# A one-core encoder layer: h turned by VectorE ahead of the gate, the gate's weight laid out piece by piece

## The chip, the cores and the metric

The kernel runs on one core of a Trainium2 chip. PE (TensorE) multiplies matrices, DVE (VectorE), ACT (ScalarE) and POOL (GpSimd) work on tiles, SP (SyncE) mostly issues transfers (DMAs). Each engine goes through its own instructions in order. The time is the device time of one execution in microseconds (us); less is better.

## The reference

One layer of a streaming encoder on 2048 + 32 rows of 1024 channels, in float32:

```
hn = rmsnorm(h, g_mix);  proj = hn @ w_in            # 1024 -> 3072
yA, yB = short gated convolution, pooling mixer      # of proj's six parts
h = h + concat([yA, yB]) @ w_out                     # 1024 x 1024
gate = sigmoid(rmsnorm(h, g_ple) @ w_ple_gate)       # 1024 x 1024
h = h + (p @ w_ple) * gate                           # p: 256 channels
return rmsnorm(h, g_final), states
```

## The kernel before

Rows come in 17 tiles: 16 of 128 rows, taken in eight pairs (0, 2, .. 14), and a short one of 32 rows (tile 16, "ol" and "gl" in names). A float32 product is made of three products of pieces: `split` (L77, L78) has ACT round a tile to its high piece and DVE subtract it for the low one. A pair's 256 x 1024 by 1024 x 1024 product is done by `seven` as seven products (the Strassen-Winograd scheme) instead of eight, each of twelve matmuls for each half. The operands of these seven are named 11, 12, 22 and S1 to S4; sums of them are tiles `fS` (L193) on DVE. Each result stays in a PSUM bank (X, Y, Z) until DVE has taken it up: `carry` makes `c_o` or `c_g` from it, `out` adds it to the row tile.

The stages, one after another:

1. The input projection and the mixers, whose result goes to DRAM transposed (`y_d`); then three early tiles of the embedding product.
2. W_out's stage. For each pair: `load_y` (L314) two y tiles, `frame_parts` makes the operands, `load_rows` (L327) the rows x, `seven` with `h_ops` (L1234) adds the product to x, `done_h` (L1260) takes the sum of squares (its root on POOL) and stores h into `h_d` on SP's queue. Meanwhile `scale_gate` (L1284 to 1289) loads the gate's weight through POOL's queue, scales it on ACT and writes `g_d`. The short tile stands between pairs 12 and 14 and goes through `plain`, whose packed products have no seven. `layout` (L1305, L1306) put W_out into its slots at the beginning.
3. The embedding stage: for 13 tiles of p, `embed`'s `prep` transposes p on PE (`ptp`, L130) and splits it, `run` multiplies it (`embed_product`, L102) and stores e into `e_d`. During it the gate's weight is read back from `g_d` (L1382) and laid out in slots of its own ("wg": `quarters`, `whole_quarters`, `weight_sums`).
4. The gate's stage, the short tile first, then the pairs. `seven` gets h as operand in transposed form. The first tile of a pair (`turned`, L1388 to 1398) is loaded from `h_d`, copied by ACT into another order (`ho`, L1394) and transposed by eight PE instructions into PSUM (`pth`, L1396). The second (`turned_here`) is loaded by four DMAs in blocks (L1405) and transposed by DVE within blocks of 32 x 32 (L1407). `prep_g` makes the operands of pair i + 2 during pair i. `gate_ops` (L1416 to 1428) applies the gate, `done_g` (L1433 to 1436) the final norm at the end of each pair, and stores the output. Pair 14 is `last_pair`.

The order on each engine is made by a scheduler which follows the program; `tc.keep_in_program_order` fixes an instruction's place, `between` hooks work into numbered steps of `seven`. Tiles come from pools with a fixed number of buffers: a new tile takes a buffer once its former tile's last reader is done, and its load waits for that. `ya` has five buffers of 128 x 1024 for y, the embedding rows and the gate's h; `xh` has three for x or h; `qa` two halves; `ring4` takes a 128 x 1024 tile from a pool.

## Time and profile before

| | us |
|---|---|
| median of 3 runs (lowest to highest) | 937.44 (936.55 to 938.89) |
| the profiled execution | 935.15 |
| its span, first to last instruction | 933.4 |
| busy in the span: PE, DVE, ACT, POOL | 917.5, 716.9, 482.2, 126.3 |

A row of the profile names an instruction or a group by its line, its engine, its operation and the tiles out<-in; numbers of buffers are left out, so `x_o` is the X bank of any W_out pair, `x_g` that of a gate pair. In brackets stands how long the engine was idle just before it, and what ended that. In the chain, "x24" is a run of 24 matmuls of one form. A table by stage gives the busy time of each engine in a stretch, with the instructions in brackets, the granted clock of TensorE (PEclk), the mean busy share of the DMA engines and the rate they moved.

### The profile page before, as it was taken

The page shows a single profiled execution, that of the slowest core. Times are in us where ns is not written, and L with a number is a line of the kernel's source. Part 1 is how long each engine was busy: PE and PEld are TensorE (multiplying, and loading weights), DVE is VectorE, ACT ScalarE, POOL GpSimd, SP SyncE. Part 2 cuts the span into 40 slices and gives each one's busy share as a digit, 9 for nine tenths or more (in the row PEclk, how much of TensorE's full clock was granted, in tenths as well). Part 3 has the DMA queues.
Part 4 walks back from the last instruction along what each step waited for, and adds up shares of the span by engine and source line. Part 5 has one row for each costly group of instructions (what it writes and reads, how often), then busy time and mean ns, then how long its engine had stood idle before and what let it go on. Part 6 is the DMA issues. An engine that isn't in the chain of part 4 may idle for free.

```text
span 933.4 us, 13100 instructions
## 1 busy us (share of the span) xinstructions
PE 917.5 (98%) x4581; PEld 827.8 (89%) x4581; DVE 716.9 (77%) x1215; ACT 482.2 (52%) x895; POOL 126.3 (14%) x244
## 2 busy tenths in 40 slices
PE   8999999899999999999999999999999999999996
PEld 7999999899999999999999987888878868888885
DVE  7997988989577868585777679665564798888985
ACT  7734564644445554443545446344334875555664
POOL 3111132211001110000000011111211001211113
PEclk9999999999999999999999999999999999999999
DMA  9357587597945547328656359766775884566563
GB/s 266 84 157 221 182 269 223 182 290 259 415 134 153 161 155 206 123 87 278 199 169 175 127 194 289 251 184 196 222 228 174 321 270 121 206 225 233 194 208 113
DMA packets 133791, 190.05 MB, mean 204 GB/s; under 512 B 11740, under 2 KB 101084, under 8 KB 132445
## 3 DMA queue, kind: packets, MB, share of 16 engines
q1 hardware_dynamic: 117741, 138.78, 47.5%
q0 software_dynamic: 13248, 44.93, 14.8%
q10 hardware_dynamic: 2736, 5.51, 1.8%
q8 instruction: 36, 0.59, 0.3%
q14 instruction: 30, 0.25, 0.1%
HBM read 129.59 MB, written 59.58 MB: 203 GB/s over the span
## 4 chain that ended last, share of the span: by engine, by line
PE 75%; DMA 2%; ACT 2%; issue 1%; DVE 1%; POOL 0%; POOLq 0%; DVEq 0%; ACTq 0%
PE x_o L167 9%; PE x_g L167 9%; PE x_zab L577 5%; PE e L102 5%; PE z_g L167 5%; PE z_o L167 4%; PE x_ch L577 4%; PE x_zbv L577 4%; PE z_zab L577 2%; PE y_g L167 2%; PE z_ch L577 2%; PE y_o L167 2%; PE b L577 2%; PE z_zbv L577 2%; PE c L577 2%; PE v L577 2%
## 5 line engine op out<-in xcount | busy, mean ns | idle before, releaser
L77 ACT CAST y_S<-y_fS 128x512 fp32r<-128x512 f32 x32 | 19.5, 622 | 43.7 <-PE x_o L167 19.2
L102 PE MATMUL e<-wq,pps 128*128 128x512 f32 (+1 forms) x156 | 38.9, 399 | 0.2 <-ACT pps L77 0.2
L167 PE MATMUL x_g<-wg_b,g_S 128*128 128x512 f32 x128 | 35.9, 390 | 0.0
L167 PE MATMUL x_o<-wo_b,y_S 128*128 128x512 f32 x128 | 35.8, 391 | 0.0
L577 PE MATMUL x_zab<-B,w_zab_S 128*128 128x416 f32 x168 | 34.6, 353 | 1.0 <-DVE w_zab_S L78 0.7
L577 PE MATMUL z_ch<-B,w_ch_S 128*128 128x416 f32 x168 | 34.3, 352 | 0.9 <-ACT U L973 0.9
L577 PE MATMUL z_zab<-B,w_zab_S 128*128 128x416 f32 x168 | 34.1, 351 | 0.5 <-ACT U L973 0.5
L577 PE MATMUL x_zbv<-B,w_zbv_S 128*128 128x416 f32 x168 | 34.2, 352 | 0.3 <-ACT zs L973 0.3
L577 PE MATMUL z_zbv<-B,w_zbv_S 128*128 128x416 f32 x168 | 34.2, 352 | 0.0
L577 PE MATMUL x_ch<-B,w_ch_S 128*128 128x416 f32 x168 | 34.1, 351 | 0.0
L102 PEld LDWEIGHTS e<-wq,pps 128*128 128x128 f32 (+1 forms) x156 | 27.4, 182 | 6.9 <-ACT pps L77 0.5
L577 PEld LDWEIGHTS x_zab<-B,w_zab_S 128*128 128x128 f32 x168 | 31.1, 188 | 2.2 <-DVE w_zab_S L78 1.0
L577 PEld LDWEIGHTS z_ch<-B,w_ch_S 128*128 128x128 f32 x168 | 31.2, 188 | 1.6 <-ACT U L973 1.2
L577 PEld LDWEIGHTS z_zab<-B,w_zab_S 128*128 128x128 f32 x168 | 31.3, 188 | 1.1 <-ACT U L973 0.8
L577 PEld LDWEIGHTS x_zbv<-B,w_zbv_S 128*128 128x128 f32 x168 | 31.3, 188 | 1.0 <-ACT zs L973 0.6
L577 PEld LDWEIGHTS x_ch<-B,w_ch_S 128*128 128x128 f32 x168 | 31.3, 188 | 0.5 <-ACT c_s L973 0.2
L577 PEld LDWEIGHTS z_zbv<-B,w_zbv_S 128*128 128x128 f32 x168 | 31.3, 188 | 0.4
L69 POOL TENSOR_SCALAR ms_f<-ssq_f 128x1 f32<-128x1 f32 (+1 forms) x15 | 8.8, 588 | 160.7 <-ACT junk L88 160.7
L77 ACT CAST y<-y 128x512 fp32r<-128x512 f32 x24 | 14.9, 620 | 28.7 <-PE z_o L167 12.8
L1435 DVE SCALAR_TENSOR_TENSOR h<-h,rstd_f,g_bc 128x1024 f32<-128x1024 f32 (+1 forms) x15 | 19.3, 1284 | 12.7 <-POOL rstd_f L73 12.7
L412 DVE SCALAR_TENSOR_TENSOR xt<-xt,rstd_x,g_bc 128x1024 f32<-128x1024 f32 (+2 forms) x14 | 17.9, 1282 | 13.9 <-POOL rstd_x L73 12.7
L167 PEld LDWEIGHTS x_o<-wo_b,y_S 128*128 128x128 f32 x128 | 24.0, 188 | 5.1 <-ACT c_o L1239 0.3
(583 smaller groups left out, 2662.5 us busy)
## 6 DMA issues: line engine op xcount, KB each, us to landing
y<-y_d SPq DMA_DIRECT2D x16, 512.0 KB, 10.2
x<-in_x_prompt_dram SPq DMA_DIRECT2D x16, 512.0 KB, 6.2
h_d<-x SPq DMA_DIRECT2D x16, 512.0 KB, 4.2
h<-h_d SPq DMA_DIRECT2D x16, 512.0 KB, 3.7
xt<-in_x_prompt_dram SPq DMA_DIRECT2D x15, 512.0 KB, 6.8
e<-e_d SPq DMA_DIRECT2D x15, 512.0 KB, 5.8
out_dram<-h POOLq DMA_DIRECT2D x14, 512.0 KB, 3.0
p_dT<-T POOLq DMA_DIRECT2D x12, 512.0 KB, 6.2
```

The lines of the kernel that those rows point to most:

```text
L69: nc.gpsimd.tensor_scalar(ms[:n], ssq[:n], scalar1=1.0 / D, scalar2=EPS, op0=ALU.mult, op1=ALU.add)
L77: ins = nc.scalar.copy(hi, src)
L102: nc.tensor.matmul(ps[:n], pps[:, a, k, :n], wp[k][b][:, cs], start=k + q == 0, stop=k == 1 and q == 2)
L167: nc.tensor.matmul(ps[:n], lhs[:, k, a, :n], w[b][:, k], start=start and k + q == 0, stop=k == KH - 1 and q == 2, skip_group_check=True)
L412: nc.vector.scalar_tensor_tensor(xt[:n], xt[:n], r[:n], g_bc[:n], op0=ALU.mult, op1=ALU.mult)
L577: nc.tensor.matmul(ps[:, :NB], lhs[:, k, x], b[:, k, y], start=start and k + q == 0, stop=stop and k == KH - 1 and q == 2, skip_group_chec ...
L1435: nc.vector.scalar_tensor_tensor(h[:n], h[:n], rf[:n], g_bc[:n], op0=ALU.mult, op1=ALU.mult)
```

## The change

- In W_out's stage each finished h tile is transposed within blocks by DVE (`turn_h`), the first of a pair at step 6 of its `seven`, the second at step 1 of the next pair, and stored on POOL's queue by four DMAs into new DRAM tiles `t_d` and `t_s`, block by block, so that the whole tile lies there transposed. `turned` in the gate's stage is then one load; the PE transposes, ACT's copies and the gate stage's DVE transposes are gone.
- `ya` is divided into `ya` with three buffers and `yb` with two, which holds the turned tiles, the embedding rows and others; `qa` holds one full tile. The y tiles of the next pair are loaded ahead of `seven`, after the x rows.
- The gate's weight is laid out into W_out's own slots, piece by piece, as they come free, from loads spread over `ya` and `xh`.
- `done_g` of a pair runs at step 1 of the next pair (`norms`).
- The embedding's p tiles are loaded two at a time; the first two are prepared at steps 3 and 4 of W_out's pair 14; the order of the last three is changed to 13, 16, 14, and the product of tile 14 is issued within the short gate tile, at `between` in `plain`.

The diff, cut to its core:

```diff
--- before.py
+++ after.py
@@ -43,6 +44,8 @@
     e_d = tc.dram_tile([T, D], F32, name="e_d")
+    t_d = tc.dram_tile([SEQ // P, P, D], F32, name="t_d")
+    t_s = tc.dram_tile([P, D // 4], F32, name="t_s")
     g_d = tc.dram_tile([D, D], F32, name="g_d")
@@ -96,12 +99,14 @@
-    def embed_product(ps, pps, wp, cs, n=P):
+    def embed_product(ps, pps, wp, cs, n=P, later=False):
         for k in range(2):
             for q, (a, b) in enumerate(((0, 0), (0, 1), (1, 0))):
-                nc.tensor.matmul(ps[:n], pps[:, a, k, :n], wp[k][b][:, cs], start=k + q == 0, stop=k == 1 and q == 2)
-
-    def embed(todo, wp, ring, queue=nc.sync):
+                ins = nc.tensor.matmul(ps[:n], pps[:, a, k, :n], wp[k][b][:, cs], start=k + q == 0, stop=k == 1 and q == 2)
+                if later:
+                    tc.keep_in_program_order(ins)
+
+    def embed(todo, wp, ring, queue=nc.sync, some=4, ahead=2):
@@ -132,18 +137,17 @@
-        def run(c, last=False):
+        def run(c, last=False, later=False):
             i = todo[c]
             r, n = tiles[i]
-            prep(c)
-            prep(c + 1)
-            prep(c + 2)
+            for a in range(ahead + 1):
+                prep(c + a)
             pps = got[c]
...
                 ps = bank(f"e_{i}_{nh}")
-                embed_product(ps, pps, wp, cs, n)
+                embed_product(ps, pps, wp, cs, n, later)
                 (nc.vector.tensor_copy if last and nh else nc.scalar.copy)(o[:n, cs], ps[:n])
@@ -272,7 +276,7 @@
-    def plain(name, A, W, n, carry, out):
+    def plain(name, A, W, n, carry, out, between=lambda: None):
@@ -280,6 +284,7 @@
         out(Z, c2, (0, 1))
+        between()
         packed(X, A[1], W["21"], n, False)
@@ -1180,12 +1185,12 @@
                 nc.sync.dma_start(g_bc, g_fin.partition_broadcast(P))
-                ya = ctx.enter_context(tc.tile_pool(name="ya", bufs=5, side="right"))
+                ya, yb = (ctx.enter_context(tc.tile_pool(name=n, bufs=b, side="right")) for n, b in (("ya", 3), ("yb", 2)))
                 first_y = load_y(0, 2 * P)
-                first_x = load_rows(ya, "x", 0, x_p)
-                tops = [ring4(ya, f"wo_q{i}") for i in range(2)]
+                tops = [ring4(yb, f"wo_q{i}") for i in range(2)]
                 for k in range(KH):
                     load_top(k, tops[k // 2])
+                first_x = load_rows(ya, "x", 0, x_p)
             if gi == 1:
@@ -1215,7 +1220,7 @@
         w3, qa, xh, st, ss, cmb = (pool(*a) for a in (
-            ("w3", 1), ("qa", 2), ("xh", 3), ("st", 4), ("ss", 3), ("cmb", 8)))
+            ("w3", 1), ("qa", 1), ("xh", 3), ("st", 4), ("ss", 3), ("cmb", 8)))
@@ -1259,8 +1264,18 @@
-        def prep_h(i):
-            lo, hi = load_y(i, 2 * P) if i else first_y
+        def turn_h(i, x):
+
+            r, n = tiles[i]
+            t = ring4(yb, f"ht_{i}")
+            tc.keep_in_program_order(nc.vector.transpose(t[:n], x[:n]))
+            g = n // 32
+            to = (t_d[i] if g == 4 else t_s).rearrange("(q c) (g n) -> g c q n", q=4, g=g)
+            for b in range(g):
+                nc.gpsimd.dma_start(to[b], t[b * 32:b * 32 + 32].rearrange("c (q n) -> c q n", q=4))
+
+        def prep_h(i, y):
+            lo, hi = y
             S[i], more = frame_parts(cmb, ss, f"y{i}", lo[:, :, :P], hi[:, :, :P], lo[:, :, P:], hi[:, :, P:])
@@ -1278,7 +1293,8 @@
-            ts = [qa.tile([P, NH], F32, tag="q", name=f"gs_{k}_{half}") for half in range(2)]
+            t = qa.tile([P, D], F32, tag="q", name=f"gs_{k}")
+            ts = t[:, :NH], t[:, NH:]
             rows = w_gate.rearrange("(q k c) n -> k q c n", q=4, k=KC)[k]
@@ -1313,8 +1329,21 @@
+
+        rest_e = [*range(EARLY, NT - 3), NT - 1, NT - 3]
+
+        def ring(what, i):
+            if what == "pps":
+                return st.tile([P, 2, 2, P], F32R, tag="t", name=f"pps_{i}")
+            if what == "out" and i not in rest_e[-LATE:]:
+                return cmb.tile([P, D], F32, tag="c", name=f"eout_{i}")
+            return ring4(yb, f"eout_{i}") if what == "out" else ss.tile([P, 2 * PLE], F32, tag="s", name=f"ep_{i}")
+
+        wq = []
+        prep, run = embed(rest_e, wq, ring, some=2)
+
         S = {}
-        more = prep_h(0)
+        more = prep_h(0, first_y)
         gate_rows = iter(range(KC))
@@ -1327,23 +1356,34 @@
                 x = [load_rows(xh, "x", i + b, x_p) for b in range(2)] if i else [first_x, second_x]
-            seven(f"o{i}", S.pop(i), W, *h_ops(x, P, f"o{i}", i == 0), {0: {1: rest}, 2: {3: next_gate}}.get(i, {}), True, i == 0)
-            for b in range(2):
-                done_h(i + b, x[b])
+                if i + 2 < NT - 1:
+                    y = load_y(i + 2, 2 * P)
+            def first_done():
+                done_h(i, x[0])
+                turn_h(i, x[0])
+
+            steps = {1: rest if i == 0 else turn_second, 3: next_gate if i == 2 else lambda: None, 6: first_done}
+            if i + 2 == NT - 1:
+                steps.update({3: partial(prep, 0), 4: partial(prep, 1)})
+            seven(f"o{i}", S.pop(i), W, *h_ops(x, P, f"o{i}", i == 0), steps, True, i == 0)
+            done_h(i + 1, x[1])
+            turn_second = partial(turn_h, i + 1, x[1])
             last = i + 4 == NT - 1
...
                 n = tiles[NT - 1][1]
-                A = short("yl", load_y(NT - 1, n), n)
+                A = short("yl", [t[:, :, :n] for t in load_y(NT - 1, n)], n)
             if i + 2 < NT - 1:
...
                 with tc.issue_after(loaded[-1].ins), tc.issue_after(hold[-1].ins):
-                    more = prep_h(i + 2)
+                    more = prep_h(i + 2, y)
                 more()
...
                 done_h(NT - 1, x)
+                turn_h(NT - 1, x)
             next_gate()
+        turn_second()
@@ -1357,55 +1397,27 @@
-        wp = embedding_chunks("wq")
-
-        rest_e = [*range(EARLY, NT - 2), NT - 1]
-
-        def ring(what, i):
-            if what == "pps":
-                return st.tile([P, 2, 2, P], F32R, tag="t", name=f"pps_{i}")
-            if what == "out" and i not in rest_e[-LATE:]:
-                return cmb.tile([P, D], F32, tag="c", name=f"eout_{i}")
-            return ring4(ya, f"e{what}_{i}")
-
-        _, run = embed(rest_e, wp, ring)
+        wq.extend(embedding_chunks("wq"))
         for c in range(len(rest_e) - LATE):
...
-        W = sums_slots("wg")
-        quarters("wg", W)
+
         for k in range(KH):
-            raw = [ring4(xh, f"wg_r{k}_{i}") for i in range(2)]
+            raw = [ring4(t, f"wg_r{k}_{i}") for i, t in enumerate(((ya, xh), (ya, ya), (xh, xh), (ya, xh))[k])]
             for i in range(2):
...
-        def turned(i):
+        def turned(i, pool=ya):
             r, n = tiles[i]
-            t = load_rows(ya, "hn", i, h_d).rearrange("p (q k c) -> p k q c", q=4, k=KC)
-            out = []
-            for half in range(2):
-                pt = tbank(f"pth_{i}_{half}")
-                o = qa.tile([P, KH, P], F32, tag="q", name=f"ho_{i}_{half}")
-                nc.scalar.copy(o[:n].rearrange("p k (q c) -> p k q c", q=4), t[:n, half * KH:half * KH + KH])
-                for k in range(KH):
-                    nc.tensor.transpose(pt[:, k * P:k * P + n], o[:n, k], ident[:n, :n])
-                out.append(pt.rearrange("p (k t) -> p k t", k=KH))
-            return out
-
-        def turned_here(i):
-
-            r, n = tiles[i]
-            t = ring4(ya, f"hn_{i}")
-            for q in range(4):
-                nc.sync.dma_start(t[q * 32:q * 32 + 32].rearrange("p (g c) -> p g c", g=4),
-                                  h_d[r:r + P, q * 256:q * 256 + 256].rearrange("(g p) c -> p g c", p=32))
-            nc.vector.transpose(t, t)
-            u = t.rearrange("p (g k t) -> p k g t", g=4, k=KC)
+            g = n // 32
+            t = pool.tile([P, D], F32, tag="t" if pool is ya else "q", name=f"hn_{i}")
+            nc.sync.dma_start(t[:, :g * 256], t_d[i] if g == 4 else t_s)
+            u = t[:, :g * 256].rearrange("p (g k t) -> p k g t", g=g, k=KC)
             return u[:, :KH], u[:, KH:]
@@ -1431,7 +1443,7 @@
             r, n = tiles[i]
-            rf = sumsq(h, n, f"f{i}")
+            rf = sumsq(h, n, f"f{i}", later=True)
             nc.vector.scalar_tensor_tensor(h[:n], h[:n], rf[:n], g_bc[:n], op0=ALU.mult, op1=ALU.mult)
@@ -1460,7 +1472,7 @@
             nc.sync.dma_start(pt, p_p[(i + 1) * P:(i + 2) * P])
-            e = load_rows(ya, "e", i, e_d)
+            e = load_rows(yb, "e", i, e_d)
             wp = embedding_chunks("wl")
@@ -1523,7 +1535,7 @@
             pps = embedded()
-            seven(f"g{i}", A, W, carry, out, {5: lambda: second(1, NH)}, first_tile=True)
+            seven(f"g{i}", A, W, carry, out, {1: norms, 5: lambda: second(1, NH)}, first_tile=True)
             second(0, NH // 2)
@@ -1531,55 +1543,61 @@
...
-            lower = []
+            upper, lower = [], []
             def first():
-                lower.extend(turned_here(i + 1))
+                upper.extend(turned(i, ya if i % 4 else qa))
+                lower.extend(turned(i + 1))
...
                 a21, a22 = lower
-                s1 = comb("S1", a21, a22, ALU.add, whole)
-                a11, a12 = turned(i)
+                s1 = comb("S1", a21, a22, ALU.add)
+                a11, a12 = upper
                 put("11", a11)
-                s2 = comb("S2", s1, a11, ALU.subtract)
-                s3 = comb("S3", whole(a11), a21, ALU.subtract, whole)
+                s2 = comb("S2", whole(s1), a11, ALU.subtract)
+                s3 = comb("S3", a11, a21, ALU.subtract)
                 put("12", a12)
-                put("S2", s2)
-                s4 = comb("S4", a12, s2, ALU.subtract)
-                put("S1", s1)
-                put("S3", s3)
-                put("S4", s4)
-                put("22", a22, whole)
+                put("S2", whole(s2))
+                s4 = comb("S4", a12, whole(s2), ALU.subtract)
+                put("S1", whole(s1))
+                put("S3", whole(s3))
+                put("S4", whole(s4))
+                put("22", a22)
...
         n = tiles[NT - 1][1]
-        A = short("gl", turned(NT - 1), n)
+        A = short("gl", [t[:, :, 0] for t in turned(NT - 1)], n)
         for step in prep_g(0).values():
             step()
-        for c in range(len(rest_e) - LATE, len(rest_e)):
-            run(c)
-        h, e = (load_rows(*a) for a in ((xh, "h", NT - 1, h_d), (ya, "e", NT - 1, e_d)))
-        plain("gl", A, W, n, *short_ops(h, e, n))
-        done_g(NT - 1, h)
+        run(len(rest_e) - LATE)
+        h, e = (load_rows(*a) for a in ((xh, "h", NT - 1, h_d), (yb, "e", NT - 1, e_d)))
+        plain("gl", A, W, n, *short_ops(h, e, n), lambda: run(len(rest_e) - 1, later=True))
+        done = [(NT - 1, h)]
+
+        def norms():
+
+            for t in done:
+                done_g(*t)
+            done.clear()
+
         for i in range(0, NT - 3, 2):
...
             h = [load_rows(xh, "h", i + b, h_d) for b in range(2)]
-            e = [load_rows(ya, "e", i + b, e_d) for b in range(2)]
-            seven(f"g{i}", A, W, *gate_ops(h, e, P, f"g{i}", i), prep_g(i + 2))
-            for b in range(2):
-                done_g(i + b, h[b])
+            e = [load_rows(yb, "e", i + b, e_d) for b in range(2)]
+            seven(f"g{i}", A, W, *gate_ops(h, e, P, f"g{i}", i), {1: norms, **prep_g(i + 2)})
+            done.extend((i + b, h[b]) for b in range(2))
         last_pair(NT - 3, S[NT - 3])
```

19 lines of the change are left out of this document (10 added, 9 removed).

## The prediction

> **What bounds the kernel now.** I read the page first: its busy times, the share of the chain that ended last, and the PE line of the 40 slices.
>
> ```profile
> span 933.4 us, 13100 instructions
> PE 917.5 (98%) x4581; PEld 827.8 (89%) x4581; DVE 716.9 (77%) x1215; ACT 482.2 (52%) x895; POOL 126.3 (14%) x244
> PE   8999999899999999999999999999999999999996
> PE 75%; DMA 2%; ACT 2%; issue 1%; DVE 1%; POOL 0%; POOLq 0%; DVEq 0%; ACTq 0%
> ```
>
> PE is busy 98% of the span, and no other engine comes above 77%. So what is taken from PE's queue comes off the time one for one, and anything else counts only where it makes PE stand. The span of 933.4 us belongs to a run of 935.15 us (1.75 us lie around the span); that run is 2.3 us below the median, 937.44. I work out a difference against the profiled run and put it on the median.
>
> Next come the stretches that the change touches: a table of busy times by stage, cut at the pairs' boundaries (a W_out pair with DVE nearly full, a usual W_out pair, the end of the embedding stage, the gate's short tile, a gate pair).
>
> ```profile
> core 0: us, PE busy (x) PEld busy (x) DVE busy (x) ACT busy (x) POOL busy (x), PEclk, DMA share, GB/s
> 553.00:570.80 17.80, 17.24 (x74) 13.47 (x74) 14.98 (x25) 9.44 (x18) 1.99 (x3) 1.00 1.07 334
> 570.80:589.80 19.00, 19.00 (x85) 15.70 (x85) 17.62 (x29) 10.22 (x18) 3.19 (x6) 1.00 0.85 270
> 609.10:628.30 19.20, 19.20 (x85) 15.67 (x85) 11.79 (x18) 7.68 (x13) 3.65 (x6) 1.00 0.74 220
> 735.00:755.40 20.40, 20.40 (x98) 15.26 (x97) 18.56 (x34) 17.47 (x38) 0.00 (x0) 1.00 0.84 299
> 755.40:763.70 8.30, 8.30 (x42) 4.86 (x41) 8.20 (x14) 5.91 (x12) 0.00 (x0) 1.00 0.91 296
> 781.07:801.03 19.96, 19.96 (x94) 16.57 (x93) 17.65 (x27) 11.69 (x21) 3.50 (x6) 1.00 0.48 158
> ```
>
> PE fills every one of these stretches at a granted clock of 1.00. DVE has 7.4 us to spare in a usual W_out pair, 2.3 in a gate pair and only 1.4 in the stretch 570.8 to 589.8, in which pair 2 of W_out begins. The same PE fills a gate pair for about 0.7 us longer than a W_out pair; PE's own timeline shows why.
>
> ```profile
> 794.51 2.88 PE L167 MATMUL x_g<-wg_b,g_S 128*128 128x512 f32 x12
> 797.23 1.30 PE L167 MATMUL z_g<-wg_d,g_S 128*128 128x512 f32 x5
> 798.37 0.60 PE L1396 MATMUL pth<-ident,ho 128*128 128x128 f32 x4
> 799.04 0.60 PE L1396 MATMUL pth<-ident,ho 128*128 128x128 f32 x4
> 800.86 1.32 PE L167 MATMUL x_g<-wg_T,g 128*128 128x512 f32 x5
> 758.19 1.03 PE L1396 MATMUL pth<-ident,ho 128*128 128x128 f32 x8
> 758.98 1.18 PE L273 MATMUL z_gl<-wg_a,gl 128*32 128x512 f32 x4
> 749.18 0.68 PE L1396 MATMUL pth<-ident,ho 32*128 32x32 f32 x8
> 749.79 5.80 PE L102 MATMUL e<-wq,pps 128*128 128x512 f32 x24
> 716.02 0.96 PE L102 MATMUL e<-wq,pps 128*128 128x512 f32 x3 [0.24 <-ACT pps L77]
> L1396 PE MATMUL pth<-ident,ho x72: 220/272/273, 749.2 to 897.3; 128*128 128x128 f32 x64, 32*128 32x32 f32 x8
> ```
>
> A product of twelve matmuls takes 797.23 − 794.51 = 2.72 us, 0.2267 each; the one with eight transposes (pth) among its twelve takes 800.86 − 797.23 = 3.63.
>
> **The change part by part: what PE gets back.** All 72 transposes go. The 64 full ones are eight groups of eight: seven stand inside pairs and cost 3.63 − 2.72 = 0.91 us each; the one in the short gate tile costs 758.98 − 758.19 = 0.79. The eight small ones cost 749.79 − 749.18 = 0.61. The embedding stage's first two preparations move into pair 14, where they fill PE as before, but the stop of 0.24 at 716.02 goes with them. Sum: 7 × 0.91 + 0.79 + 0.61 + 0.24 = 8.0 us. Matmul counts are otherwise equal. The last embedding product moves into the short tile with nothing added; there it covers the preparation of the gate's pair 0.
>
> **What DVE gets instead.** Its transpose exists in the trace, eight times in the gate stage, and so does every other kind of row that is moved.
>
> ```profile
> L1407 DVE STREAM_TRANSPOSE hn<-hn x8: 1235/1236/1239, 756.1 to 895.2; 128x1024 f32<-128x1024 f32 x8
> 580.47 0.68 DVE L1234 TENSOR_TENSOR c_o<-x_o,x 128x512 f32<-128x512 f32 x1
> 581.07 0.68 DVE L78 TENSOR_TENSOR y_S<-y_fS,y_S 128x512 fp32r<-128x512 f32 x1
> 620.36 0.68 DVE L1234 TENSOR_TENSOR c_o<-z_o,x 128x512 f32<-128x512 f32 x1
> 573.33 2.88 PE L167 MATMUL x_o<-wo_c,y 128*128 128x512 f32 x12
> 609.09 5.44 PE x_o L167 x24
> 628.30 5.44 PE x_o L167 x24
> ```
>
> Two transposes of 1.24 us go into each W_out pair: 11.79 + 2.47 = 14.3 of 19.2, which fits; 17 in all, less the eight that leave the gate's pairs, where 17.65 − 1.24 = 16.4 stands against a pair of 19.05. The other DVE operations start 0.60 apart (581.07 − 580.47).
>
> The Trainium skill ("VectorE: DVE Perf Modes", The three transpose paths) says that DVE only transposes within blocks of 32 × 32, and its Rules for kernel authors would leave a 128 × 128 transpose on TensorE when it can write PSUM. By that rule the work stays on PE and the gain is nothing, so 937.4; the rows above decide against it here, since DVE has 7.4 us free per pair and PE none.
>
> **What the turned tiles add around DVE.** Each full tile adds four stores on POOL's queue, 65 in all with the short tile's one. In exchange 41 loads on SP become 17.
>
> ```profile
> 587.40 0.69 POOL L1284 DMA_DIRECT2D gs<-in_w_ple_gate_dram x1 [5.05 <-DMA g_d<-gs]
> 597.43 0.73 POOL L1284 DMA_DIRECT2D gs<-in_w_ple_gate_dram x1 [4.07 <-DMA g_d<-gs]
> ```
>
> At 0.73 us an issue (597.43), eight stores are 5.8 us per pair on an engine that is busy 3.65 of 19.2. Queued behind a scaled-weight load they can wait 5.05 us, and the ring of turned tiles has two places, so the tile two later waits for them a whole pair on: hidden. They add 1 MB per 19.2 us, an estimate of 55 GB/s on top of 220.
>
> The stores carry a second risk, for the input tiles. Five buffers become three for y plus two for the turned tiles, so a y tile is loaded about one pair ahead and its buffer comes free late. The landing times bound this.
>
> ```profile
> 571.80 0.33 SPq L1260 DMA_DIRECT2D h_d<-x  x1
> 609.84 0.32 SPq L1260 DMA_DIRECT2D h_d<-x  x1
> DMA to landing us min/median/max: 6.1/10.2/14.2
> x<-in_x_prompt_dram SPq DMA_DIRECT2D x16, 512.0 KB, 6.2
> h_d<-x SPq DMA_DIRECT2D x16, 512.0 KB, 4.2
> e<-e_d SPq DMA_DIRECT2D x15, 512.0 KB, 5.8
> ```
>
> (The third row is that of the y loads.) *Pair 2.* The second y tile of pair 4 takes the buffer of the first x tile, which must be stored first: 571.80 + 4.2 = 576.0. It lands at 582.1 with the shortest landing, 6.1. In the new DVE order its first sum and a split stand ahead of the second carry of pair 2 (c_o). PE wants that carry done when the third X product starts. By the new PE order that is 573.33 plus forty matmuls of 0.2267, at 582.4. DVE reaches it at 582.1 + 0.60 + 0.60 + 0.69 = 584.0: a stall of 1.6 us at 6.1, 5.7 at the median of 10.2, and up to 9.7 at 14.2; nothing if the load is a little quicker or DVE's order gives way. The 6.1 and the 14.2 are the only two y landings that can be told apart in time; the stretches are those at 270 and at 334 GB/s. The new stretch has pair 2's traffic, so it is nearest to 6.1: I take 2.0.
>
> *Usual W_out pairs (4 to 10).* A second y tile is issued behind an x load on SP that waits for a store: 609.84 + 4.2 = 614.0, so at about 614.4. DVE wants it at 621.0 (the carry from z at 620.36 is just ahead). What PE needs behind it is the sum that frees X for the last product at 628.30, three operations later (0.60 + 0.60 + 0.69 = 1.9). So the load may take 628.3 − 1.9 − 614.4 = 12.0 us; above that each us costs one in each of four pairs. With 220 + 55 = 275 GB/s, as in the stretch that gave 6.1, I take 0; the largest landing, 14.2, would give 4 × 2.2 = 8.8.
>
> The Trainium skill has a fit ("DMA: Bandwidth & Descriptors", Anatomy of one DMA — SWDGE (gpsimd) path) of about 2.0 us plus the bytes over 436 GB/s. For a tile of 512 KB that is an estimate of 3.2 us, and by it no y load would be late. The rows of the y loads, 6.1 at the least on SP's queue, do not bear that out.
>
> **The gate's weight.** Its layout goes from the embedding stage into W_out's own slots, as the last products of pair 14 and the embedding stage release them. In the stretch 735 to 764 DVE and ACT were nearly full with it (18.56 of 20.4, 8.20 of 8.30) and PE stood for none of it. It now starts within pair 14, ahead of that pair's first carry in DVE's order. One load of weight rows must land for that; a late load would hold PE. Bounds: nothing, as in the stretch named, to 2 us, about what the load of the pair's last x tile has to spare; I take 0, because pair 14's stretch has light traffic.
>
> **The gate's pairs.** Norms a pair later take DVE's waits for the root off no chain of PE's.
>
> ```profile
> L1435 DVE SCALAR_TENSOR_TENSOR h<-h,rstd_f,g_bc 128x1024 f32<-128x1024 f32 (+1 forms) x15 | 19.3, 1284 | 12.7 <-POOL rstd_f L73 12.7
> 787.84 0.69 DVE L1427 TENSOR_TENSOR e<-e,c_g 128x512 f32<-128x512 f32 x1 [0.41 <-ACT c_g L1425]
> ```
>
> These waits (12.7 us over 15 norms, 0.85 each) go on beside PE. Two buffers for the embedding rows make their loads wait for the pair before. They are first read 787.84 − 781.07 = 6.8 us into a pair, and land in 5.8: about 1 us to spare. Cost 0, up to 1 us in each of seven pairs if that is gone. The last pair and the tail are untouched.
>
> **Sum:** −8.0 + 2.0 = −6.0 us. The profiled run would be 935.15 − 6.0 = 929.2, and the median 937.44 − 6.0 = 931.4.
>
> **The rivals.** *A, all covers hold:* no stall in pair 2, −8.0, so 929.4. For it: DVE's order is met within a pair that has 1.4 us of slack, and the price hangs on one landing; against it: 6.1 is the shortest landing seen. *B, the other side, late y loads:* with three buffers every second y tile lands late, DVE stands at its first sum in order, and PE waits. For a landing of L the losses are (L − 4.5) in pair 2 and 4 × (L − 12.0) in the usual pairs; at 14.2 they are 9.7 + 8.8 = 18.5, less 8.0: +10.5, so 947.9. It loses to before from L = 12.1 on. For it: median 10.2 and the added stores; against it: DMA is below 0.85 in these pairs. *C, the gain is spent elsewhere:* embedding rows or the weight's layout hold PE about 1 us in seven pairs, or the loads take the median 10.2 in pair 2 and pair 14 loses its 2 us: −8.0 + 7 or −8.0 + 5.7 + 2, so about 936.8. For it: margins of 1 to 2 us in every place; against it: none of these waits was seen on PE.
>
> **How the numbers follow.** Forecast, with pair 2 losing 0.5 to 4 us: 0.41. A: 0.20. C: 0.18, of which 0.02 still fast. B: 0.21. A measurement here tells about 0.3%, 2.8 us, from no change: faster is below 934.6, slower above 940.3. So faster 0.41 + 0.20 + 0.02 = 0.63; same 0.16; slower 0.21. The forecast's own range is 929.9 to 933.4. For 8 in 10 the range takes in A and C and the near end of B: 928.8 to 940.5.
>
> **What would show it.** No pth rows, and gate pairs 19.0 to 19.1 apart in the chain, show the gain; a DVE transpose of about 1.24 us, 17 times within the W_out stage, shows where it went. PE idle with DVE's c_o as releaser between 575 and 592 shows pair 2's stall, 1.6 to 4 us of it. DVE idle behind a y load at the first sum (L197), with W_out pairs over 19.3, would be B. Embedding-row loads releasing DVE in the gate's pairs, or PE idle at 696 to 708 or in the short gate tile, would be C. The forecast is wrong if W_out pairs lengthen by over 1 us each, or if gate pairs do not shorten to 19.1.

## The result and the profile after

The changed kernel takes 945.33 us (median of 6 runs, 943.78 to 947.24) against 937.22 before (6 runs): the ratio is 1.0089, with a 95% interval of 1.0078 to 1.0100. It is slower by about 8 us, where 6 us less was forecast. Its profiled execution took 946.43 us, with a span of 944.6 us; so the differences between the two profiles, 11.2 us in all, are about 3 us larger than that between the medians (before's profile lies 2.3 us below its median as quoted in the forecast, this one 1.1 above).

The page of the changed kernel, the lines that answer to those shown of before:

```profile
span 944.6 us, 13051 instructions
PE 914.9 (97%) x4509; PEld 822.1 (87%) x4509; DVE 726.6 (77%) x1224; ACT 472.9 (50%) x877; POOL 160.7 (17%) x309
PE   8999999999999999999999999999999899999995
PEclk9999999999999999999999999999999899999998
```

PE does less work, 914.9 against 917.5 us, but stands for longer: 944.6 − 914.9 = 29.7 us of the span against 15.9. One slice in the 32nd place has lost both busy time and clock. The view of PE's waits, summed over the run (total, times, longest), names what it stood for; these four rows have no counterpart of their size before:

```profile
PE ptp L135 <- DVE pps L81: 4.2, 1, 4.2
PE x_o L171 <- DVE c_o L1239: 3.3, 4, 1.6
PE x_o L171 <- DVE x L1239: 2.0, 1, 2.0
PE z_g L171 <- ACT c_g L1428: 1.2, 1, 1.2
```

The next table is worked out from PE's timeline of the two profiles: each stage runs from its first product to the next stage's first (the transposes of p tiles are not counted as its start).

| stage, us | before | after | difference |
|---|---|---|---|
| up to W_out's first product | 552.9 | 553.8 | +0.9 |
| W_out's stage | 163.1 | 170.5 | +7.4 |
| embedding stage (13 products, then 12) | 39.4 | 42.5 | +3.1 |
| short gate tile (then with one embedding product) | 8.3 | 10.1 | +1.9 |
| gate pairs, until pair 12 and the last pair's first product are done | 142.6 | 136.3 | −6.3 |
| rest of the last pair, to PE's end | 19.3 | 21.0 | +1.7 |
| PE's end to the span's end | 7.8 | 10.4 | +2.5 |

One embedding product moved by 2.97 us from one stage to the other, where it takes 2.74. Without that the embedding stage lost 6.1 us and the short tile gained 0.9. The first row is work that the change does not touch; over all kernels of this study it lies between 552.8 and 556.9, and what moves it is not explained.

**Where the gain is.** The gate pairs gained 6.3 us. The timeline of PE in the changed kernel shows the product that held the eight transposes before:

```profile
787.85 2.88 PE L171 MATMUL x_g<-wo_b,g_S 128*128 128x512 f32 x12
790.57 2.88 PE L171 MATMUL z_g<-wo_d,g_S 128*128 128x512 f32 x12
793.28 2.90 PE L171 MATMUL x_g<-wo_T,g 128*128 128x512 f32 x12
```

It takes 793.28 − 790.57 = 2.71 us instead of 3.63.

**Where the embedding stage lost.** ACT's, DVE's and PE's timelines and a table of PE around the stop (busy time, clock, DMA share and rate):

```profile
743.98 0.62 ACT L80 CAST wo_c<-wg_r 128x512 fp32r<-128x512 f32 x1 [6.31 <-DMA wg_r<-g_d]
744.63 0.69 DVE L81 TENSOR_TENSOR wo_d<-wg_r,wo_c 128x512 fp32r<-128x512 f32 x1 [6.23 <-ACT wo_c L80]
745.84 0.42 DVE L81 TENSOR_TENSOR pps<-ptp,pps 128x256 fp32r<-128x256 f32 x1
746.31 0.69 PE L135 MATMUL ptp<-ident,ep 128*128 128x128 f32 x2 [4.16 <-DVE pps L81]
746.65 5.44 PE L105 MATMUL e<-wq,pps 128*128 128x512 f32 x12
752.06 3.01 PE L105 MATMUL e<-wq,pps 128*128 128x512 f32 x12
```

```profile
741.00:745.00 4.00, 1.15 (x6) 1.00 0.95 367
745.00:749.00 4.00, 2.69 (x8) 0.51 0.55 221
749.00:753.00 4.00, 4.00 (x14) 0.64 0.92 288
```

ACT stands for 6.31 us for a load of the gate's weight. DVE stands behind ACT, with the split of the next p tile (pps) in its queue after the weight's split, so PE has nothing to multiply for 4.16 us. The load was issued at 733.14 and its tile first read at 743.98, 10.8 us later, with a DMA share of 1.00 on the way (733.1 to 744). Afterwards the granted clock is 0.51 and 0.64, and a product that takes 3.01 takes 5.44.

**Where W_out's stage lost.** First pair 2, then pair 8, from the timelines of SP, DVE and PE:

```profile
571.97 0.69 DVE L197 TENSOR_TENSOR y_fS<-y,y 128x512 f32<-128x512 f32 x1 [1.75 <-DMA y<-y_d]
578.04 2.14 PE L171 MATMUL z_o<-wo_a,y_S 128*128 128x512 f32 x8 [0.54 <-DVE y_S L81]
583.94 0.69 DVE L197 TENSOR_TENSOR y_fS<-y,y 128x512 f32<-128x512 f32 x1 [1.22 <-DMA y<-y_d]
585.89 3.02 PE L171 MATMUL x_o<-wo_b,y_S 128*128 128x512 f32 x12 [1.05 <-DVE c_o L1239]
632.28 2.98 PE L171 MATMUL x_o<-wo_T,y 128*128 128x512 f32 x12
637.61 0.32 SPq L1265 DMA_DIRECT2D h_d<-x  x1
638.08 5.37 SPq L332 DMA_DIRECT2D x<-in_x_prompt_dram  x2
643.54 1.22 SPq L319 DMA_DIRECT2D y<-y_d  x1
651.62 0.69 DVE L197 TENSOR_TENSOR y_fS<-y,y 128x512 f32<-128x512 f32 x1 [4.41 <-DMA y<-y_d]
653.78 3.00 PE L171 MATMUL x_o<-wo_T,y 128*128 128x512 f32 x12 [1.99 <-DVE x L1239]
```

In both places the first sum of a coming pair waits for a y tile, and PE waits behind it. In pair 2 this happens twice: at 571.97 for pair 2's own second y tile (DVE then has no gap until 582.7, and PE stops for 0.54 and 0.27 us), and at 583.94 for that of pair 4 (1.05 us). The last W_out pair has a third stop, 1.57 us at 708.8, where the first weight split stands ahead of the pair's carry.

**Where the end lost.** The rows of POOL's drain, the last long instruction on its queue, at the program's end (durations shortest/middle/longest in ns), before and after:

```profile
L1609 POOLq DRAIN  x3: 40/93/2822, 928.5 to 933.1; - x3
```

```profile
L1627 POOLq DRAIN  x3: 40/93/6993, 936.9 to 944.4; - x3
```

It takes 7.0 us instead of 2.8, while the last output was issued at 938.25 and such stores land within 2.4, and no later work stands in the profile.

### The profile page after: what moved, and what is told of

It reads as the page before. It is cut to its first block, busy times and chain, and to the rows that moved or that the text cites. A ratio compares the mean times of both kernels' runs of the same rounds, so it can differ in the third digit from the quotient of the medians.

```text
span 944.6 us, 13051 instructions
## 1 busy us (share of the span) xinstructions
PE 914.9 (97%) x4509; PEld 822.1 (87%) x4509; DVE 726.6 (77%) x1224; ACT 472.9 (50%) x877; POOL 160.7 (17%) x309
## 5 line engine op out<-in xcount | busy, mean ns | idle before, releaser
L105 PE MATMUL e<-wq,pps 128*128 128x512 f32 (+1 forms) x156 | 40.9, 416 | 0.0
L1275 POOL DMA_DIRECT2D t_d<-ht x64 | 36.2, 570 | 2.3 <-DVE ht L1271 1.8
L171 PE MATMUL x_g<-wo_b,g_S 128*128 128x512 f32 x128 | 35.7, 389 | 0.0
L80 ACT CAST g_S<-g_fS 128x512 fp32r<-128x512 f32 x32 | 19.7, 620 | 23.7 <-PE x_g L171 11.2
L171 PEld LDWEIGHTS x_g<-wo_b,g_S 128*128 128x128 f32 x128 | 24.0, 188 | 5.0
```

The lines of the kernel that those rows point to most:

```text
L80: ins = nc.scalar.copy(hi, src)
L105: ins = nc.tensor.matmul(ps[:n], pps[:, a, k, :n], wp[k][b][:, cs], start=k + q == 0, stop=k == 1 and q == 2)
L171: nc.tensor.matmul(ps[:n], lhs[:, k, a, :n], w[b][:, k], start=start and k + q == 0, stop=k == KH - 1 and q == 2, skip_group_check=True)
L1275: nc.gpsimd.dma_start(to[b], t[b * 32:b * 32 + 32].rearrange("c (q n) -> c q n", q=4))
```

## The experiments

All times are medians with the ratio to the kernel before on the same chip and its 95% interval. The stage lengths are found as in the table above, each in the one profiled execution of its kernel. Executions of one kernel spread by 1.5 to 8.4 us (e12: 935.9 to 944.3), so a difference of 1 to 3 us between two stages is not resolved.

| kernel | time, us | ratio | W_out | embedding | gate, to PE's end | POOL's drain |
|---|---|---|---|---|---|---|
| before | 937.2 | 1 | 163.1 | 39.4 | 161.9 | 2.8 |
| changed | 945.3 | 1.0089 (1.0078 to 1.0100) | 170.5 | 42.5 | 157.3 | 7.0 |
| e1, weight's layout as before | 944.0 | 1.0070 (1.0053 to 1.0086) | 170.2 | 39.5 | 157.8 | 7.0 |
| e2, norms as before | 946.0 | 1.0093 (1.0076 to 1.0109) | 172.6 | 37.9 | 157.1 | 7.0 |
| e3, stores on SP | 964.2 | 1.0284 (1.0256 to 1.0311) | 186.8 | 42.3 | 157.2 | 2.8 |
| e4, no turning | 934.6 | 0.9962 (0.9948 to 0.9975) | 168.3 | 35.6 | 157.2 | 2.8 |
| e5, transposes without stores | 933.2 | 0.9954 (0.9939 to 0.9970) | 166.8 | 35.6 | 157.3 | 2.8 |
| e11, no turning, five shared buffers | 931.6 | 0.9930 (0.9914 to 0.9946) | 164.2 | 35.6 | 158.0 | 2.8 |
| e8, half the tiles, five shared buffers | 949.5 | 1.0124 (1.0104 to 1.0143) | 179.0 | 36.7 | 157.4 | 4.6 |
| e12, stores in whole rows | 938.9 | 1.0016 (0.9997 to 1.0036) | 173.4 | 36.0 | 157.2 | 3.7 |
| e13, no stores of tiles 14 and 15 | 941.9 | 1.0044 (1.0029 to 1.0058) | 170.4 | 35.8 | 157.3 | 6.3 |
| e9, whole rows, four loads | 947.7 | 1.0102 (1.0081 to 1.0122) | 169.9 | 37.1 | 166.7 | 3.7 |
| e10, e9's stores on ACT | 954.8 | 1.0180 (1.0164 to 1.0195) | 177.3 | 36.0 | 163.8 | 2.8 |
| e6, before, DVE for all in the gate | 952.4 | 1.0155 (1.0137 to 1.0173) | 163.2 | 39.3 | 176.5 | 2.8 |
| e7, e6 with sums on POOL | 962.8 | 1.0269 (1.0251 to 1.0287) | 163.2 | 39.4 | 188.7 | 2.8 |

My first theory was that three things cost the time, each from its own part of the change: the y buffers (W_out's stage), the weight's layout (embedding stage), and the norms (last pair). The rival was that the turned tiles cost it, by DVE's time or by their stores.

**The parts undone one by one.** e1 gives the gate's weight its own slots again:

```diff
+        W = sums_slots("wg")
+        quarters("wg", W)
         for k in range(KH):
-            raw = [ring4(t, f"wg_r{k}_{i}") for i, t in enumerate(((ya, xh), (ya, ya), (xh, xh), (ya, xh))[k])]
+            raw = [ring4(xh, f"wg_r{k}_{i}") for i in range(2)]
```

> The changed kernel, with the gate's weight again laid out in slots of its own and its raw rows loaded into xh alone, as before the change. Theory L (the piece-by-piece layout, whose loads wait for the last h tiles, holds ACT and DVE in order and so PE for 4.2 us, after which the clock is low): the embedding stage from the first product to the short gate tile falls from 42.5 to about 36 us, PE's stop in pair 14 of 1.6 us goes, the time falls from 945.3 by 6 to 8 us to about 938. Rival (the loads from xh are late in any case, since DVE is behind from the turned tiles): a stop of 3 us or more stays in the embedding stage, time within 2 us of 945.

944.0: neither. PE's stop in the embedding stage shrinks from 4.16 to 2.11 us but does not go, and W_out's stage is the same; the stop in pair 14 is gone. The layout in pieces is not the cause by itself: with the old layout DVE, too, stands for a load of the gate's weight (6.36 us, until 735.57).

e2 puts the norms back to the end of each pair:

```diff
-            seven(f"g{i}", A, W, *gate_ops(h, e, P, f"g{i}", i), {1: norms, **prep_g(i + 2)})
+            seven(f"g{i}", A, W, *gate_ops(h, e, P, f"g{i}", i), prep_g(i + 2))
             done.extend((i + b, h[b]) for b in range(2))
+            norms()
...
```

> The changed kernel with the final norms at the end of each pair again. Theory N (norms put off into the last pair hold its carries): PE's stop of 1.2 us in the last pair goes and PE ends about 2 us sooner after the last pair's first product; time 943.4. Rival (the last pair is late because of the turned operands, not the norms): time 945.3, the stop stays.

946.0. The stop in the last pair is 0.53 instead of 1.16 us, and the rest of the last pair after its first product 20.1 instead of 21.0, but the pairs before are 0.8 longer and the gate's stage is as long as in the changed kernel (157.1 against 157.3): theory N is half right in the last pair, and nothing is gained by it. In this execution the embedding stage's stop is 1.89 us (stage 37.9), though stores and layout are those of the changed kernel, and W_out's stage is 172.6; so the size of the stop also hangs on the order of work or on the execution, and its 4.16 us is not a fixed price.

e3 stores the turned tiles through SP:

```diff
-                nc.gpsimd.dma_start(to[b], t[b * 32:b * 32 + 32].rearrange("c (q n) -> c q n", q=4))
+                nc.sync.dma_start(to[b], t[b * 32:b * 32 + 32].rearrange("c (q n) -> c q n", q=4))
```

> The changed kernel with the 65 stores of turned tiles issued on SP's queue instead of POOL's. Theory P (POOL's stores lengthen the end, where POOL's drain took 7.0 us instead of 2.8): the stretch from PE's last matmul to the end falls from 10.4 to about 8 us; W_out's stage may lose 0 to 4 us since x and y loads now queue behind stores that wait for a transpose; time 943 to 947. Rival (the drain has nothing to do with the stores): the end stays at 10 us or more.

964.2. The drain is back at 2.8 us: the long drain comes of POOL's stores. W_out's stage lost 16 us more, four times what I allowed: on SP the x and y loads stand in order behind stores that wait for a transpose.

**The turning taken away.** In e4 `turn_h` returns at once and the gate loads rows of h:

```diff
         def turn_h(i, x):
             r, n = tiles[i]
-            t = ring4(yb, f"ht_{i}")
...
+            return
...
-            nc.sync.dma_start(t[:, :g * 256], t_d[i] if g == 4 else t_s)
+            nc.sync.dma_start(t[:, :g * 256], h_d[r:r + n] if g == 4 else h_d[r:r + n].rearrange("r (a c) -> (r a) c", a=4))
```

> The changed kernel without the turning: no DVE transposes and no stores of turned tiles in W_out's stage; the gate's operands are loaded from the rows of h as they are, so they are not transposed and the gate's values are not the reference's. Buffers and all else as in the changed kernel. W_out's stage took 170.5 us in the changed kernel against 163.1 before. Theory Y (three y buffers make the y loads late): the stage keeps 4 us or more of its loss, about 168, time about 943. Rival D (the transposes in DVE's order, or the stores' traffic, cause it): the stage falls to 165 or less, time about 939.

934.6, 10.7 us under the changed kernel. W_out's stage keeps 5.2 of its 7.4 us, as theory Y has it; but the embedding stage is down to 35.6, with no stop of PE in it, although the layout is that of the changed kernel. So the rival holds for the embedding stage, which is why theory Y's time of 943 was missed, and theory Y for most of W_out's.

e5 keeps the transposes and drops only their stores:

```diff
-            for b in range(g):
-                nc.gpsimd.dma_start(to[b], t[b * 32:b * 32 + 32].rearrange("c (q n) -> c q n", q=4))
```

(and loads as in e4).

> The changed kernel with the DVE transposes in W_out's stage but without their 65 stores; the gate's operands are loaded from the rows of h as they are, so the gate's values are not the reference's. Without transposes and stores together the time was 934.6, the embedding stage 35.6 us (42.5 in the changed kernel) and W_out's stage 168.3 (170.5). Theory S (the stores' traffic delays the loads of weight rows and x): with the transposes alone the embedding stage is about 36, W_out's about 168.5, the end about 8, time 935 to 936. Rival D (the two transposes of pair 14 and those in each pair hold DVE): embedding stage 40 or more, W_out's 170 or more, time 941 or more, with only the end's 2.4 us regained.

933.2, as theory S has it. DVE's 17 transposes of 1.23 us cost nothing that can be seen; the 65 stores cost 945.3 − 933.2 = 12.1 us (the gate's stage, whose loads differ, is 157.3 in both). The page of e5 and PE's waits in it from W_out's stage on:

```profile
span 931.7 us, 12920 instructions
PE 910.8 (98%) x4509; PEld 820.5 (88%) x4509; DVE 727.4 (78%) x1224; ACT 472.2 (51%) x877; POOL 123.7 (13%) x244
```

```profile
PE x_o L171 <- DVE c_o L1239: 1.7, 2, 1.4
PE z_o L171 <- DVE y_S L81: 1.5, 1, 1.5
PE z_g L171 <- ACT c_g L1426: 1.1, 1, 1.1
PE y_o L166 <- ACT wo_c L1319: 0.5, 1, 0.5
```

DVE is as busy as in the changed kernel (727.4 against 726.6), and the stop of 4.2 us is gone.

e11 gives e4 one pool of five buffers instead of three and two:

```diff
-                ya, yb = (ctx.enter_context(tc.tile_pool(name=n, bufs=b, side="right")) for n, b in (("ya", 3), ("yb", 2)))
+                ya = yb = ctx.enter_context(tc.tile_pool(name="ya", bufs=5, side="right"))
```

> The changed kernel without turning (as before: the gate's operands are not transposed), and with ya and yb one pool of five buffers. With three and two it took 934.6, W_out's stage 168.3 against 163.1 before the change. Theory Y (three y buffers cost some 4 us there): W_out's stage 164 to 165, time about 931. Rival (the loads moved ahead of the seven, or the weight's layout in pair 14, cost it): stage 167 or more.

W_out's stage is 164.2 and the time 931.6: theory Y. The two buffers set apart cost 168.3 − 164.2 = 4.1 us there and 3 us of the time (ratios of 0.9962 and 0.9930, on two chips).

**Which property of the stores.** e12 stores a turned tile by one DMA in rows of 4 KB and loads it back by one:

```diff
-            for b in range(g):
-                nc.gpsimd.dma_start(to[b], t[b * 32:b * 32 + 32].rearrange("c (q n) -> c q n", q=4))
+            if g == 4:
+                nc.gpsimd.dma_start(t_d[i], t)
...
```

> The changed kernel with each turned tile stored by one POOL DMA in rows of 4 KB (17 stores, the same bytes) and loaded back by one DMA as it stands, so the gate gets blocks in a wrong order and its values are not the reference's; unlike the kernel with four loads per tile, the gate's loads are as many as in the changed kernel. Theory Q (the embedding stage's loss comes of the stores' small pieces and many issues, W_out's of their bytes): W_out's stage 170, embedding stage about 37, gate to the last pair 133.3, drain 3.7, time about 938.5. Rival B (the bytes do all of it): embedding stage 40 or more, time 942 or more.

The embedding stage is 36.0, the drain 3.7, the time 938.9, all as theory Q has them. W_out's stage is not better (173.4, and 169.9 in e9, which has the same stores): larger pieces gain nothing that can be seen there. So the same bytes in 17 large stores spare the embedding stage's stop and most of the drain; size and number of the stores are changed together and not told apart. How they spare the stop is only in part shown: the load that ACT waits for still takes 9.1 us (issued at 734.66, read at 743.73) against 10.8, but it goes out 6.4 us into the stage instead of 8.9. Why it goes out sooner is not settled.

e13 leaves out only the last eight stores:

```diff
-            for b in range(g):
+            for b in range(g if i not in (14, 15) else 0):
...
```

> The changed kernel without the eight stores of the turned tiles 14 and 15, the last of W_out's stage (their gate operands are loaded from the rows of h, not transposed, so the gate's values of these two tiles are not the reference's). Theory C (these stores, on the way while the weight's rows are loaded for the layout, make the load late on which ACT, DVE and then PE stand): embedding stage about 36, W_out's stage unchanged at 170, drain 6.5, time about 938. Rival (what is late has built up over the whole W_out stage, the gate's weight scaled too late): embedding stage 40 or more, time 943 or more.

The embedding stage is 35.8: theory C, in the profiled execution. There the load that ACT waits for takes 6.5 us (731.75 to 738.26) instead of 10.8, so the eight stores of tiles 14 and 15, issued from 726.6 to 732.8 in the changed kernel, make it late. The time, 941.9, lies between the two forecasts (938 and 943 or more): the runs of this kernel spread from 938.3 to 943.8, and the profiled one, 938.4, is among the quickest; what the slower ones lose, and whether the stop returns in them, is not shown. The rows of ACT in e13, first for the same split as the one at 743.98 in the changed kernel, then for a later one:

```profile
738.26 0.62 ACT L80 CAST wo_c<-wg_r 128x512 fp32r<-128x512 f32 x1 [2.62 <-DMA wg_r<-g_d]
743.50 0.62 ACT L80 CAST wo_c<-wg_r 128x512 fp32r<-128x512 f32 x1 [0.54 <-DMA wg_r<-g_d]
```

**Kernels meant to keep the gain and lose the cost.** e9 makes e12 whole: the blocks are put in order by four loads per tile in the gate's stage.

```diff
-            nc.sync.dma_start(t[:, :g * 256], t_d[i] if g == 4 else t_s)
+            for q in range(4):
+                if g == 4:
+                    nc.sync.dma_start(t[q * 32:q * 32 + 32].rearrange("c (g n) -> c g n", g=4),
+                                      t_d[i][:, q * 256:q * 256 + 256].rearrange("(g c) n -> c g n", c=32))
...
```

> The changed kernel with each turned tile stored by one DMA in rows of 4 KB, as it stands, still on POOL's queue (17 stores instead of 65, the same bytes, a quarter of the row pieces); the reordering of blocks moves to the gate's loads, four per tile in pieces of 1 KB. Theory Q (the small pieces and the four issues of the stores hold the DMA engines and POOL): W_out's stage 167, embedding stage about 36, POOL's drain 2.82 + 17 times 0.064 = 3.9 us, time about 934.5. Rival B (the bytes do it): W_out's stage 170, embedding stage 40 or more, time 941 or more, less only the drain's 3 us.

The drain is 3.7 and the embedding stage 37.1, as theory Q has them; W_out's stage, 169.9, is rival B's. But the time is 947.7: the gate lost 9.4 us. The longest of DVE's waits in its gate stage, a row that stood at 1.4 us in 7 times in the changed kernel:

```profile
DVE e L1445 <- ACT c_g L1443: 18.4, 19, 1.4
```

With four loads per tile instead of one the scheduler set the gate's operands and carries in another order, and PE stops about 1 us in each pair for a split of g_S. Why it did so is not settled. e12, whose gate loads are as many as in the changed kernel, has a gate of 157.2.

e10 issues e9's stores from ACT (`nc.scalar.dma_start(t_d[i], t)`).

> As the last, with these 17 stores on ACT's queue: no POOL store is added. Theory P: drain 2.8 us and an end of 7.8 us, so 1 us under the last kernel if ACT has room. Rival: ACT stands for the transposes in order and its casts come late; W_out's stage 2 us or more above the last kernel's.

The drain is 2.8 us as theory P has it, and W_out's stage is 177.3, 7 us above e9's, as the rival has it, and the time 954.8. ACT stands for transposes, 2.3 and 1.9 us by the profile; PE's two longest stops there are 2.55 and 2.98 us, with a low clock after each. That the first makes the second is argued, not shown.

e8 turns only the first tile of each pair in W_out's stage and shares five buffers:

```diff
-            turn_second = partial(turn_h, i + 1, x[1])
+            turn_second = lambda: None
...
-                lower.extend(turned(i + 1))
+                lower.extend(turned_here(i + 1))
```

(with e11's pool, and `turned_here` of before).

> The changed kernel with only the first tile of each pair turned in W_out's stage (8 transposes and 32 stores besides the short tile's) and the second again in the gate's stage, and with ya and yb one pool of five buffers. Theory Y and S (buffers and store traffic make the losses): W_out's stage about 166, embedding stage 36 to 38, time 934 to 938. Theory P (each POOL store adds some 64 ns to POOL's drain at the end, from 65 stores and 4.17 us): drain 2.82 + 33 times 0.064 = 4.9 us. Rival: drain 7.0 or 2.8, and W_out's stage 170.

949.5. The drain, 4.6 us, lies between the others as expected. W_out's stage is the longest but one, 179.0: in a shared pool y tiles take buffers that wait for a turned tile's stores (the second y load of most pairs waits for the semaphore of such a store), and DVE stands 26.3 us for y loads. The forecast for that stage was wrong by 13 us, that for the time by 11 or more.

e6 does the transposes alone, on before, in the gate's stage:

```diff
-                lower.extend(turned_here(i + 1))
+                upper.extend(turned_here(i))
+                lower.extend(turned_here(i + 1))
...
-                a11, a12 = turned(i)
+                a11, a12 = upper
...
```

> The kernel before with one part of the change alone: no PE transposes of full tiles, but the first tile of each gate pair loaded in blocks and transposed by DVE in the gate's stage, as the second already is; all else as before (buffers, layout, norms, stores). Theory G (each group of eight PE transposes costs 0.9 us and nothing else is needed): gate pairs of 19.05, time 937.2 - 7 = 930. Rival (DVE, then 18.9 of 19.05 us busy in a gate pair, becomes the bound): pairs of 20 us or more, time 937 or more.

952.4: the rival, in its time. The gate lost 14.6 us, with PE waiting mostly for ACT's casts of g_S (13.3 us in four stops). e7 moves four sums of a pair to POOL (`nc.gpsimd.tensor_tensor(hh, hh, ee, op=ALU.add)`).

> As the last, with the four sums h + e of a gate pair (and of the short tile) on POOL instead of DVE: 2.8 us less on DVE, some 5.1 us (4 times 1.28) more on POOL, which is busy 3.5 of 20. Theory G with room on DVE: about 930, and not above the last kernel. Rival (POOL's sums take part in the chains to the norms and the tail, or slow DVE): above the last kernel by 1 us or more.

962.8: room on DVE did not help, and POOL's sums cost 10 us more. So these two ways of leaving out the way round W_out's stage, with its stores, cost more than it does. No version in this study that computes the whole reference beats the kernel before.

## Why the prediction was wrong

*What PE gets back: right.* 7 × 0.91 = 6.4 was forecast for the gate pairs, 6.3 measured. The short tile gained 0.9 where 0.79 stood. The small transposes and the short stop were worth 0.85; in e5, whose stores are gone, the embedding stage is 35.6 against 39.4 − 2.97 = 36.4, so 0.8.

*What DVE gets instead: right.* "Two transposes of 1.24 us go into each W_out pair ... which fits." e5 has them and is 4 us faster than before.

*Pair 2: the step right, its stop half the size, the total luck.* A stall of 2.0 us was forecast behind the second y tile of pair 4. That tile was issued at 577.46 and read at 583.94 (576.0 and 582.1 were forecast), and the stop behind it is 1.05. The stops of 0.54 and 0.27 came earlier, behind pair 2's own second y tile, issued at 563.61 (555.21 before), which the forecast did not have; that all three together make 1.9 us is luck. The pair is 2.8 us longer; each start after a stop costs some 0.3 more, which the estimate left out.

*Usual W_out pairs: the step failed that set the load's issue.* It took the x load ahead on SP to wait for the first store of a pair (609.84 + 4.2). In the run the two x loads stood at 638.08 for 5.37 us, until the pair's second store (637.61) had landed, so the y load went out 643.54 − 632.28 = 11.3 us after the start of the last product of the pair before (the mark that is 609.09 in the forecast) instead of 5.3. It then took 8.1 us, 19.4 in all. By the forecast's own rule, 5.3 + 12.0 = 17.3 us were free; the excess of 2.1 is the stop of 1.99 in pair 8. This is rival B's wait, at a landing of 8.1 and not 12.1. Pairs 4 to 12 lost 3.2 us together, where 0 was taken.

*Pair 14: mis-sized within its bounds.* 0 was taken, the bound was 2; the stop is 1.57.

*The gate's weight: the step that failed most.* It bounded a late weight load by nothing to 2 us, and from the stretch where before DVE and ACT were full and PE did not stand. What differs is the traffic: the last turned tiles' stores are on the way with the loads. It cost 6.9 us in the profiled execution, 42.5 against 35.6 in e5: a stop of 4.16 and about 2.5 for the low clock after it. The "light traffic" of the forecast is that of pair 14 before (a DMA share of 0.46 from 696 to 716); the load that was late went out in the embedding stage, at a share of 1.00 (733.1 to 744). Rival C named the weight's layout, at 1 to 2 us in pair 14 or the gate; no rival had this price or the clock.

*The stores on POOL: the step "hidden" failed.* It weighed POOL's issue time and the two places of the ring, and left out both what their traffic does to the last loads of the stage and POOL's drain at the end, 4.2 us longer, of which 2.5 show in the span. "The last pair and the tail are untouched" failed with it. The last pair also lost 1.7 us; its stop of 1.1 us is in e5 and e11 too, where nothing is stored, and 0.53 with the norms of before: neither stores nor buffers cause it; with the norms of before (e2) this stretch is 0.9 us shorter, so they account for about half of the 1.7, and the rest stays open.

*The account.* The gain was forecast as 8.0 us and is 6.3 + 0.9 + 0.8 = 8.0. The losses were forecast as 2.0 and are 7.4 in W_out's stage, 6.9 in the embedding stage, 1.7 in the last pair, 2.5 at the end and 0.9 ahead of all this; 19.4 − 8.0 = 11.4, and the moved product takes 0.2 less in its new place, which makes the 11.2 between the profiles. Two readings in the forecast are loose, and neither moves its sum: PE fills 17.24 of 17.80 us of the first stretch, and the two figures for the weight's layout are DVE's, ACT's being 17.47 of 20.4 and 5.91 of 8.30.

The sum by the study's own kernels: e11, without turning and with five buffers, is 931.6, by chance the forecast's number; two buffers set apart add 3 (e4), the transposes nothing (e5), the stores 12.1. The Trainium skill's fit in the section Anatomy of one DMA — SWDGE (gpsimd) path of "DMA: Bandwidth & Descriptors" would land 512 KB in an estimated 3.2 us; the y loads of 512 KB in the changed kernel, on SP's queue, took 4.5 to 8.0 us, longer than the fit in every case.

## What to carry to other kernels

A transpose moved off the bounding engine is paid for by its way through DRAM: price its stores by what else is on the way at their time, above all where a stage ends and the next one's weights load. Where an engine is in order, one late load stops everything behind it, so look for what stands behind each wait on every engine in the chain (here ACT, then DVE, then PE), and price the clock after a long stop as well. Buffers set apart for a new use are taken from an old one, and that use's loads go out later.

## What the runs showed of the hardware

POOL's drain at the end grows with the number of stores that POOL has issued, though in the changed kernel the last of these was issued 204 us ahead of it (732.8): 2.82 us with none of the turned tiles' stores, 3.73 with 17 (e12), 4.62 with 33 (e8), 6.34 with 57 (e13) and 6.99 with 65, so 53 to 64 ns each. The longest rows in e12, e8 and e13, in this order:

```profile
L1631 POOLq DRAIN  x3: 40/93/3725, 934.2 to 939.1; - x3
```

```profile
L1637 POOLq DRAIN  x3: 40/93/4623, 940.8 to 946.6; - x3
```

```profile
L1627 POOLq DRAIN  x3: 40/102/6338, 929.5 to 936.4; - x3
```

It does not go by bytes: e12 stores as many as the changed kernel.

After long stops of PE the granted clock was low for one to two stretches of 4 us: 0.51 and 0.64 at the 4.16 us in the changed kernel, and in e1 after 2.11 us 0.63 in the next stretch:

```profile
733.00:737.00 4.00, 1.89 (x10) 1.00 1.03 374
737.00:741.00 4.00, 4.00 (x13) 0.63 1.02 407
```

From W_out's stage on, the fifteen profiles have 25 stops of 1.8 us or more. After all eleven of 2.76 us or more the clock fell to 0.50; of the fourteen from 1.84 (e12) to 2.69 us (e6) it fell after seven and stayed at 1.00 after seven, among them 1.99 us in the changed kernel (at 653.8) and 2.61 us in e8; after none of 1.2 to 1.75 us did it fall. The Trainium skill ("TensorE: Matmul & The Clock Gate", Part 1: The HAM clock gate) puts the fall after an idle window of about 3.4 us; here it came after 1.84 us already, and the measurement decides.
